# A decoder trunk on one Trainium2 core: down and output products as 2x2 blocks with seven block products

## The chip, the core and the metric

The kernel runs on one core of one Trainium2 chip. The metric is the device time of one execution in microseconds (us); the median of three runs of the kernel before is 1233.89 us (1233.36 to 1233.97). All shapes are fixed: 512 positions, model width 1024, FFN width 2816, 16 heads, fp32 inputs.

Engines are called PE (TensorE), DVE (VectorE), ACT (ScalarE), POOL (GpSimd) and SP (SyncE, whose queue issues the transfers). The built program holds a list of instructions for each engine; the pieces of these lists shown below are called order rows.

## The reference, cut to what matters

```python
def short_conv_mixer(xn, w_in, conv_w, w_out):
    b, c, h = jnp.split(xn @ w_in, 3, axis=-1)
    u = causal_dwconv(c * h, conv_w)
    return (b * u) @ w_out

def conv_ffn(xn, w_up, conv_w, w_down):
    a, g = jnp.split(xn @ w_up, 2, axis=-1)
    a = causal_dwconv(a, conv_w)
    return (jax.nn.silu(a) * g) @ w_down

# layer 0: x += short_conv_mixer(rmsnorm(x)); x += conv_ffn(rmsnorm(x))
# then shared K, V and a forget gate from rmsnorm(x)
# layer 1: x += forgetting_attention(q(rmsnorm(x)), k, v, c); x += conv_ffn(rmsnorm(x))
```

The products that the change rewrites are `@ w_out` of the mixer (1024x1024) and `@ w_down` of both FFNs (2816x1024), each on 512 positions.

## The kernel before

Everything is kept transposed: a tile has 128 channels on the partitions and 512 positions along the free dimension. The stages follow one another: the mixer's input product (24 output tiles from `a_in`), its output product (8 tiles from `a_out`), FFN 0's up product (22 values of j, for each a tile a and a tile g), its down product (8 output tiles, 22 blocks of K each), keys, values and attention, `b_out`, then FFN 1 in the same way.

fp32 products are made of fp32r passes. Each weight and each activation is split into a high part, rounded to fp32r, and a low part, the remainder. For each block of K of 128 and each half of 256 positions PE runs three matmuls of 128x256: high by high, high by low and low by high (`mac`, L130 to L132). So one output tile with 8 blocks of K (`gemm`) is 48 matmuls.

A piece of weights is loaded with 8 blocks of K (512 KB) into one of three buffers `wraw`. Then, 512 columns at a time, ACT rounds the high part (L110) and DVE subtracts it to get the low part (L111), into four buffers of a pool of their own, `wsp`. One gemm so has two casts on ACT and two subtractions on DVE. Activations are split by `split` (cast L162 on ACT, subtraction L163 on DVE or POOL).

In the up stage each j runs: gemm of a, L316 on DVE (a times the norm's factor r), the convolution (L241 on ACT, L242 and L244 on DVE), SiLU (L192 on ACT), gemm of g, L322 on DVE (g times r), L323 on POOL (g times y), and the split (L162, L163). The down stage then runs the 8 gemms with 22 blocks of K, and x is added by L271 on DVE. In the mixer, L292 to L302 play the part of L316 to L323, and x is written to DRAM (`xsp`) only after FFN 0's down stage, tile by tile.

Nobody writes the order of the queues by hand: a scheduler places the instructions, and it hands out the buffers of a pool in the order in which the program asks for them. In the program before, `wsp` belongs to the weights alone, and `f`-like products and their splits come from other pools.

Of the kernel before, what the change touches and what calls it, by code (L numbers as in the profile page):

```python
# [52 lines left out]
def trunk(ctx: ExitStack, tc: tile.TileContext, x_t, a_in, a_out, up0, down0, wk, wv, wf, wqg, b_out,  # L54
# [78 lines left out]

    def gemm(src, xs, nk=KT):

        ps = mmps()
        for k, w in enumerate(weights(src, nk)):
            mac(ps, w, xs[k], k == 0, k == nk - 1)
        return ps

    def gemm2(srcs, xs, hold=1):

        pss, kept = [], []
        for src in srcs:
            ps = mmps()
            late = []
            for k, w in enumerate(weights(src)):
                if k < KT - hold:
# [5 lines left out]
        for ps, late in zip(pss, kept):  # L154
            for k, w in late:
                mac(ps, w, xs[k], False, k == KT - 1)
# [80 lines left out]

    def conv(src, col):
# [9 lines left out]
    def back(m):  # L248
        t = new(misc, "ld", [P, T], F32, bufs=3)
        nc.sync.dma_start(out=t, in_=xsp[m])  # L250
        return t

    def project(src, hs, nk, norm, last=False, spilled=False, spill=False, pss=()):

        for m in range(KT):
            if m < len(pss):
                ps = pss[m]
            elif nk == KT and m < 2:
# [3 lines left out]
            else:  # L262
                ps = gemm(src[m], hs, nk)
# [615 lines left out]
```

## Time and profile before

| what | value |
| --- | --- |
| median of three runs | 1233.89 us (1233.36 to 1233.97) |
| the profiled execution's own time | 1233.1 us |
| span of the profiled execution, first to last instruction | 1231.3 us |
| PE busy | 1216.5 us, 99% of the span, 10425 matmuls |
| DVE, ACT, POOL busy | 678.6, 537.4 and 203.1 us |
| mean granted clock of TensorE | 0.996 |

A share of 99% for PE says that TensorE is nearly always at work over the whole program; the pipelined matmuls overlap in the records, so the length of one record is more than the distance from one matmul to the next. A granted clock of 1 is TensorE's upper level, 2.4 GHz, and 0.5 is 1.2 GHz. In a row of the timeline the first number is the start in the span, the second the duration, and the bracket at the end names the idle time before it and what ended it.

### The profile page before, as it was taken

Reading aid. Unit: us, or ns where it says so; the run is one execution under the profiler, and the core shown is the slowest. Engines: PE = TensorE matmul, PEld = TensorE weight load, DVE = VectorE, ACT = ScalarE, POOL = GpSimd, SP = SyncE. Lnnn points to the kernel's source line nnn. Section 1 sums busy time; section 2 is a strip of 40 time slices with the busy share of each in tenths; the row PEclk is TensorE's granted clock in tenths of the full one; section 3 lists DMA queues with packets and bytes.
Section 4 is the critical chain, followed back from the end, with each engine's and each line's share of the span. In section 5 each row is a group of like instructions: output and inputs, shape, how many; then the busy total and the mean of one; then the engine's idle time right before and its main releaser. Section 6 shows DMA issues by size and latency. Waiting matters only on the chain.

```text
span 1231.3 us, 24568 instructions
## 1 busy us (share of the span) xinstructions
PE 1216.5 (99%) x10425; PEld 1189.0 (97%) x10425; DVE 678.6 (55%) x1163; ACT 537.4 (44%) x973; POOL 203.1 (16%) x181
## 2 busy tenths in 40 slices
PE   9999999999999999999999899999999999999998
PEld 8999999999999999999998788889999999999998
DVE  6755556555555533344646787876565555553222
ACT  5433345334333433333556767775543334342221
POOL 0100021111111100000123435442111111110000
PEclk9999999999999999999999999999999999999999
DMA  6233233333333344342342212124233233233341
GB/s 215 87 103 101 88 104 92 97 104 93 97 104 91 93 130 125 121 140 87 95 139 79 84 52 86 53 87 129 86 104 101 89 103 101 89 99 104 116 119 45
DMA packets 39374, 124.14 MB, mean 101 GB/s; under 512 B 4384, under 2 KB 4896, under 8 KB 39264
## 3 DMA queue, kind: packets, MB, share of 16 engines
q1 hardware_dynamic: 38048, 120.41, 31.8%
q10 hardware_dynamic: 1152, 1.97, 0.5%
q8 instruction: 81, 1.33, 0.4%
q14 instruction: 29, 0.24, 0.1%
q0 software_dynamic: 64, 0.20, 0.0%
HBM read 118.33 MB, written 4.23 MB: 100 GB/s over the span
## 4 chain that ended last, share of the span: by engine, by line
PE 90%; ACT 4%; DVE 3%; POOL 2%; issue 1%; DMA 0%; SPq 0%; DVEq 0%; POOLq 0%; ACTq 0%
PE st L131 18%; PE st L130 17%; PE st L132 17%; PE mm L130 11%; PE mm L132 11%; PE mm L131 11%; ACT s L189 1%; PE st L620 1%; PE at L658 1%; PE st L649 1%; POOL m L667 1%; DVE s L624 1%; DVE wlo L111 1%; ACT g L189 1%; ACT g L162 1%
## 5 line engine op out<-in xcount | busy, mean ns | idle before, releaser
L130 PE MATMUL st<-g,whi 128*128 128x256 f32 x1686 | 465.5, 276 | 0.0
L131 PE MATMUL st<-g,whi 128*128 128x256 f32 x1686 | 465.4, 276 | 0.0
L132 PE MATMUL st<-g,wlo 128*128 128x256 f32 x1686 | 465.4, 276 | 0.0
L110 ACT CAST whi<-wraw 128x512 fp32r<-128x512 f32 (+1 forms) x394 | 240.4, 611 | 473.6 <-PE st L131 291.9
L111 DVE TENSOR_TENSOR wlo<-wraw,whi 128x512 fp32r<-128x512 f32 (+1 forms) x394 | 283.6, 720 | 222.9 <-ACT whi L110 218.3
L130 PE MATMUL mm<-g,whi 128*128 128x256 f32 x1242 | 346.2, 279 | 0.0
L131 PE MATMUL mm<-g,whi 128*128 128x256 f32 x1242 | 343.5, 277 | 0.0
L132 PE MATMUL mm<-g,wlo 128*128 128x256 f32 x1242 | 343.5, 277 | 0.0
L130 PEld LDWEIGHTS st<-g,whi 128*128 128x128 f32 x1686 | 316.6, 188 | 0.1
L131 PEld LDWEIGHTS st<-g,whi 128*128 128x128 f32 x1686 | 316.5, 188 | 0.1
L132 PEld LDWEIGHTS st<-g,wlo 128*128 128x128 f32 x1686 | 316.5, 188 | 0.0
L130 PEld LDWEIGHTS mm<-g,whi 128*128 128x128 f32 x1242 | 233.5, 188 | 1.8
L131 PEld LDWEIGHTS mm<-g,whi 128*128 128x128 f32 x1242 | 233.4, 188 | 1.3
L132 PEld LDWEIGHTS mm<-g,wlo 128*128 128x128 f32 x1242 | 233.2, 188 | 0.1
L323 POOL TENSOR_TENSOR m<-m,m 128x512 f32<-128x512 f32 x44 | 69.1, 1573 | 408.3 <-DVE m L322 370.9
L162 ACT CAST g<-m 128x512 fp32r<-128x512 f32 x66 | 40.8, 619 | 90.4 <-POOL m L323 66.8
L163 DVE TENSOR_TENSOR g<-m,g 128x512 fp32r<-128x512 f32 x51 | 36.8, 722 | 67.3 <-ACT g L162 66.7
L224 POOL TENSOR_TENSOR m<-m,m 128x512 f32<-128x512 f32 x21 | 27.9, 1330 | 175.5 <-ACT m L222 153.6
L640 POOL TENSOR_SCALAR s<-s,sm 128x128 f32<-128x128 f32 (+3 forms) x64 | 41.4, 660 | 75.5 <-DVE sm L637 69.2
L189 ACT ACTIVATE s<-s,bb 128x128 f32<-128x128 f32 (+3 forms) x64 | 35.4, 555 | 22.9 <-DVE bb L633 22.8
L241 ACT ACTIVATE m<-m,pr 128x512 f32<-128x512 f32 x52 | 37.7, 725 | 15.9 <-DVE m L316 13.0
L242 DVE SCALAR_TENSOR_TENSOR m<-m,pr,m 128x511 f32<-128x511 f32 x52 | 39.0, 750 | 9.5 <-ACT m L241 9.5
(170 smaller groups left out, 1312.3 us busy)
## 6 DMA issues: line engine op xcount, KB each, us to landing
wraw<-up SPq DMA_DIRECT2D x88, 512.0 KB, 3.5
wraw<-down SPq DMA_DIRECT2D x32, 448.0 KB, 3.5
wraw<-a_in SPq DMA_DIRECT2D x21, 512.0 KB, 3.6
wraw<-down SPq DMA_DIRECT2D x16, 512.0 KB, 3.5
wraw<-wqg SPq DMA_DIRECT2D x16, 512.0 KB, 3.6
wraw<-a_out SPq DMA_DIRECT2D x8, 512.0 KB, 3.5
ld<-xsp SPq DMA_DIRECT2D x16, 256.0 KB, 2.8
wraw<-wv SPq DMA_DIRECT2D x8, 512.0 KB, 3.6
```

Of the source, the lines that this page charges most:

```text
L110: nc.scalar.copy(out=hi[:, :n], in_=raw)
L111: nc.vector.tensor_tensor(out=lo[:, :n], in0=raw, in1=hi[:, :n].bitcast(F32), op=ALU.subtract)
L130: nc.tensor.matmul(ps[:, f], lhsT=lh[0], rhs=rh[0][:, f], start=go, stop=False, skip_group_check=True)
L131: nc.tensor.matmul(ps[:, f], lhsT=lh[0], rhs=rh[1][:, f], start=False, stop=False, skip_group_check=True)
L132: nc.tensor.matmul(ps[:, f], lhsT=lh[1], rhs=rh[0][:, f], start=False, stop=end, skip_group_check=True)
L162: nc.scalar.copy(out=hi, in_=src)
L163: (eng or nc.vector).tensor_tensor(out=lo, in0=src, in1=hi.bitcast(F32), op=ALU.subtract)
L189: chain["exp"] = ordered(nc.scalar.activation(**kw), chain["set"])
L241: nc.scalar.activation(out=y, in_=src, func=AF.Copy, scale=pr[:, col + 2:col + 3])
L242: nc.vector.scalar_tensor_tensor(out=y[:, 1:T], in0=src[:, 0:T - 1], scalar=pr[:, col + 1:col + 2], in1=y[:, 1:T], op0=ALU.mult, op1=ALU.add)
L323: nc.gpsimd.tensor_tensor(out=g, in0=g, in1=y, op=ALU.mult)
L640: nc.gpsimd.tensor_scalar(out=s, in0=s, scalar1=sm[:, e:e + 1], scalar2=1.0, op0=ALU.mult, op1=ALU.mult)
```

## The change

The three products become 2x2 block products in Winograd's form. Two K blocks of the activation (two tiles of j, or of i in the mixer) and the two halves of 256 positions give one operand of four blocks; two output tiles m and two K blocks of weights give the other. Seven block products, each of n pairs of K blocks, take the place of eight. For that

- `operands` makes from each pair of tiles, in the wide tile `f`, three sums of blocks on DVE (L250, L252, L253), and splits all of them (ACT L257 three times and L262, DVE L258 three times and L263);
- `Seven.prepare` makes the sums of the weights on POOL (L281 1024 or 768 columns wide, L283 and L284 half as wide) and splits raw weights and sums (ACT L290, DVE L291);
- `Seven.go` runs the products (L305 to L307), and the outputs are put together by copies on ACT (L318, L320, L324) and additions on POOL and DVE (L321, L325, L326, L335 to L337, L425);
- the down stage runs in three parts, with 3, 4 and 4 pairs, after the gemm of g of j=6 and j=14, and at the end. Between the parts x lies in DRAM: each part loads its tiles of x (`ld`) and stores the sum (`xsp`). `Project` prepares the first `Seven` of a part when it is made, ahead of the gemms of j=6, 14 and 21.

The pools `wraw`, `wsp`, `sp` and `ptp` become one pool `wide` of 18 tiles of 128x1024. Raw weights, their high and low parts, `f` and the sums `t` of `operands`, and tiles of the attention all come from it. Weights are split 1024 columns at a time (L113 on ACT, L114 on DVE, once per gemm instead of twice). In all gemms that stay, the matmuls are L131 to L133. Lines that have moved: L316 is now L484, L322 L490, L323 L496, L241 L343, L242 L344, L244 L346, L192 L195. The program has 10113 matmuls after 10425 before; those of 128x256 go from 9792 to 9480.

```diff
-    big = ctx.enter_context(tc.tile_pool(name="big", bufs=58))
-    sp = ctx.enter_context(tc.tile_pool(name="sp", bufs=10))
-    ptp = ctx.enter_context(tc.tile_pool(name="ptp", bufs=6))
+    big = ctx.enter_context(tc.tile_pool(name="big", bufs=52))
-    wraw = ctx.enter_context(tc.tile_pool(name="wraw", bufs=3))
-    wsp = ctx.enter_context(tc.tile_pool(name="wsp", bufs=4))
+    wide = ctx.enter_context(tc.tile_pool(name="wide", bufs=18))
...
+    def W(dtype=F32):
+        return new(wide, "w", [P, 2 * T], dtype)
...
-        hi = new(wsp, "whi", [P, T], F32R)
-        lo = new(wsp, "wlo", [P, T], F32R)
-        nc.scalar.copy(out=hi[:, :n], in_=raw)
-        nc.vector.tensor_tensor(out=lo[:, :n], in0=raw, in1=hi[:, :n].bitcast(F32), op=ALU.subtract)
+        hi, lo = W(F32R), W(F32R)
+        nc.scalar.copy(out=hi[:, :n], in_=raw[:, :n])
+        nc.vector.tensor_tensor(out=lo[:, :n], in0=raw[:, :n], in1=hi[:, :n].bitcast(F32), op=ALU.subtract)
...
+    def operands(f):
+        t, v = W(), blocks(f)
+        tv = blocks(t)
+        nc.vector.tensor_tensor(out=tv[:, 0:2], in0=v[:, 0:4:3], in1=v[:, 1:2].to_broadcast([P, 2, HT]),
+                                op=ALU.subtract)
+        nc.vector.tensor_tensor(out=tv[:, 2], in0=tv[:, 1], in1=v[:, 0], op=ALU.add)
+        nc.vector.tensor_tensor(out=tv[:, 3], in0=tv[:, 2], in1=v[:, 2], op=ALU.subtract)
+        ops = {}
+        for names, src in (("57", tv[:, 0:2]), ("13", v[:, 0:4:3]), ("64", tv[:, 2:4])):
+            hi, lo = G(F32R), G(F32R)
+            nc.scalar.copy(out=blocks(hi), in_=src)
+            nc.vector.tensor_tensor(out=blocks(lo), in0=src, in1=blocks(hi).bitcast(F32), op=ALU.subtract)
...
+        g = G(F32R)
+        nc.scalar.copy(out=g[:, 0:HT], in_=v[:, 2])
+        nc.vector.tensor_tensor(out=g[:, HT:T], in0=v[:, 2], in1=g[:, 0:HT].bitcast(F32), op=ALU.subtract)
...
+    class Seven:
...
+        def prepare(self):
+            b, (r0, r1) = self.b, self.raw
+            s, s2 = W(), W()
+            nc.gpsimd.tensor_tensor(out=blocks(s[:, 0:2 * b], b), in0=blocks(r0[:, 0:2 * b], b),
+                                    in1=blocks(r1[:, b:2 * b], b).to_broadcast([P, 2, b]), op=ALU.add)
+            nc.gpsimd.tensor_tensor(out=s2[:, 0:b], in0=s[:, 0:b], in1=r0[:, b:2 * b], op=ALU.add)
+            nc.gpsimd.tensor_tensor(out=s2[:, b:2 * b], in0=s2[:, 0:b], in1=r1[:, 0:b], op=ALU.add)
+            self.w = {}
+            for names, raw in (("14", r0), ("2", r1), ("75", s), ("63", s2)):
+                n = len(names) * b
+                hi = W(F32R)
+                lo = hi[:, n:2 * n] if len(names) == 1 else W(F32R)
+                nc.scalar.copy(out=hi[:, 0:n], in_=raw[:, 0:n])
+                nc.vector.tensor_tensor(out=lo[:, 0:n], in0=raw[:, 0:n], in1=hi[:, 0:n].bitcast(F32), op=ALU.subtract)
...
+        def go(self, names, xs, ks):
...
+            for m in names:
...
+                for p in ks:
...
+                    nc.tensor.matmul(ps, lhsT=wh, rhs=xh, start=m in "57" and p == 0, stop=False, skip_group_check=True)
+                    nc.tensor.matmul(ps, lhsT=wh, rhs=xl, start=False, stop=False, skip_group_check=True)
+                    nc.tensor.matmul(ps, lhsT=wl, rhs=xh, start=False, stop=p == self.n - 1, skip_group_check=True)
...
+    class Project:
+        def __init__(self, src, n):
+            self.src, self.n = src, n
+            self.sevens = {}
+            self.load(0)
+            self.load(1)
+            self.sevens[0].prepare()
...
         for j in range(JT):
+            if j in parts_ or j == JT - 1:
+                n = min(c for c in parts_ if c >= j) // 2 - k0
+                part = Project([z[:, 4 * k0 * P:4 * (k0 + n) * P] for z in down], n)
...
-            nc.gpsimd.tensor_tensor(out=g, in0=g, in1=y, op=ALU.mult)
-            if j < 5:
-                us.append(split(g, new(sp, "s", [P, T], F32R), new(sp, "s", [P, T], F32R)))
-            else:
-                us.append(split(g))
-        project(down, us, JT, nxt, last, spill=spill)
+            if j in parts_:
+                part.run(us, None)
+                us, k0 = [], k0 + n
+            if j % 2 == 0:
+                f = W()
+            nc.gpsimd.tensor_tensor(out=half(f, j), in0=g, in1=y, op=ALU.mult)
+            if j % 2:
+                us.append(operands(f))
+        part.run(us, nxt, last=last, hold=True)
```

**The end of an even j in the up stage.** DVE's order rows before, for the end of the gemm of g of one j (L322 waits for it) and the start of the next; `whi` and `wlo` are the halves of a weight piece, a new piece has a new `wraw`, and PE reads wlo_3290 in the first half of the next gemm.

```order
L111 TENSOR_TENSOR wlo_3290<-wraw_3287,whi_3289 128x512
L322 TENSOR_TENSOR m_3213<-st_3154,r_2405 128x512
L111 TENSOR_TENSOR wlo_3318<-wraw_3287,whi_3317 128x512
L163 TENSOR_TENSOR g_3217<-m_3213,g_3216 128x512
L111 TENSOR_TENSOR wlo_3356<-wraw_3353,whi_3355 128x512
L316 TENSOR_TENSOR m_3279<-st_3220,r_2405 128x512
```

The change, DVE, for the end of g of j=2 (L490) and the a of j=3, whose low part is w_2668; w_2730 is the low part of the g of j=3.

```order
L484 TENSOR_TENSOR m_2598<-mm_2543,r_2384 128x512
L344 SCALAR_TENSOR_TENSOR m_2600<-m_2598,pr,m_2600 128x511
L346 SCALAR_TENSOR_TENSOR m_2600<-m_2598,pr,m_2600 128x510
L490 TENSOR_TENSOR m_2660<-st_2605,r_2384 128x512
L114 TENSOR_TENSOR w_2668<-w_2665,w_2667 128x1024
L114 TENSOR_TENSOR w_2730<-w_2727,w_2729 128x1024
L484 TENSOR_TENSOR m_2719<-st_2664,r_2384 128x512
```

The low part of the next gemm's weights stood ahead of L322, and now stands behind L490.

**The end of an odd j.** DVE's order rows of the change from the end of g of j=3 (L490) on; w_2807 is the low part of the weights of the a of j=4, and w_2662 is `f`.

```order
L490 TENSOR_TENSOR m_2781<-st_2726,r_2384 128x512
L250 TENSOR_TENSOR w_2784<-w_2662 128x512
L252 TENSOR_TENSOR w_2784<-w_2784,w_2662 128x256
L253 TENSOR_TENSOR w_2784<-w_2784,w_2662 128x256
L258 TENSOR_TENSOR g_2789<-w_2784,g_2788 128x512
L258 TENSOR_TENSOR g_2793<-w_2662,g_2792 128x512
L258 TENSOR_TENSOR g_2797<-w_2784,g_2796 128x512
L263 TENSOR_TENSOR g_2800<-w_2662,g_2800 128x256
L114 TENSOR_TENSOR w_2807<-w_2804,w_2806 128x1024
L114 TENSOR_TENSOR w_2869<-w_2866,w_2868 128x1024
L484 TENSOR_TENSOR m_2858<-st_2803,r_2384 128x512
```

On ACT before, around the SiLU (L192) and the cast of one j's product (L162 into s_2688):

```order
L241 ACTIVATE m_2621<-m_2619,pr 128x512
L110 CAST whi_2761<-wraw_2759 128x512
L192 ACTIVATE m_2621<-m_2621 128x512
L110 CAST whi_2789<-wraw_2759 128x512
L162 CAST s_2688<-m_2685 128x512
L110 CAST whi_2827<-wraw_2825 128x512
L110 CAST whi_2855<-wraw_2825 128x512
```

On ACT in the change, from the convolution and SiLU (L343, L195) of j=3 on; w_2806 is the high part of the weights of the a of j=4, w_2868 that of its g.

```order
L343 ACTIVATE m_2721<-m_2719,pr 128x512
L195 ACTIVATE m_2721<-m_2721 128x512
L257 CAST g_2788<-w_2784 128x512
L257 CAST g_2792<-w_2662 128x512
L257 CAST g_2796<-w_2784 128x512
L262 CAST g_2800<-w_2662 128x256
L113 CAST w_2806<-w_2804 128x1024
L113 CAST w_2868<-w_2866 128x1024
L343 ACTIVATE m_2860<-m_2858,pr 128x512
```

Before, one cast L162 stood between the casts of weights; now the four casts of `operands`, of which the first and the third wait for DVE's L250 and L253, stand ahead of L113, and L250 waits for POOL's L496. In before, the DVE rows at this place are those of the even j, since each j is alike there.

**The entry of a part.** On POOL in the change, around j=5, whose product is the second L496 into w_2922; L281 to L284 into w_3071 and w_3072 are the sums of the first `Seven` of the part, those into w_3210 and w_3211 of the second. Before, POOL has only L323 here, one for each j.

```order
L496 TENSOR_TENSOR w_2922<-m_2920,m_2860 128x512
L496 TENSOR_TENSOR w_2922<-m_3041,m_2981 128x512
L281 TENSOR_TENSOR w_3071<-w_3063,w_3064 128x768
L283 TENSOR_TENSOR w_3072<-w_3071,w_3063 128x384
L284 TENSOR_TENSOR w_3072<-w_3072,w_3064 128x384
L281 TENSOR_TENSOR w_3210<-w_3067,w_3068 128x768
L283 TENSOR_TENSOR w_3211<-w_3210,w_3067 128x384
```

On DVE in the change, at the same place, from the last splits of `operands` on; w_3095 is the low part of the weights of the a of j=6, w_3157 that of its g.

```order
L258 TENSOR_TENSOR g_3057<-w_3044,g_3056 128x512
L263 TENSOR_TENSOR g_3060<-w_2922,g_3060 128x256
L291 TENSOR_TENSOR w_3077<-w_3063,w_3076 128x768
L291 TENSOR_TENSOR w_3080<-w_3064,w_3080 128x384
L291 TENSOR_TENSOR w_3084<-w_3071,w_3083 128x768
L291 TENSOR_TENSOR w_3088<-w_3072,w_3087 128x768
L114 TENSOR_TENSOR w_3095<-w_3092,w_3094 128x1024
L114 TENSOR_TENSOR w_3157<-w_3154,w_3156 128x1024
L291 TENSOR_TENSOR w_3216<-w_3067,w_3215 128x768
L291 TENSOR_TENSOR w_3219<-w_3068,w_3219 128x384
```

All four splits of the first `Seven`, of which the last two wait for POOL's sums, have come ahead of the next gemm's L114.

## Rows read from the trace of the kernel before

**Rows 1.** The page: span, busy times, chain by engine.
```profile
span 1231.3 us, 24568 instructions
PE 1216.5 (99%) x10425; PEld 1189.0 (97%) x10425; DVE 678.6 (55%) x1163; ACT 537.4 (44%) x973; POOL 203.1 (16%) x181
PE 90%; ACT 4%; DVE 3%; POOL 2%; issue 1%; DMA 0%; SPq 0%; DVEq 0%; POOLq 0%; ACTq 0%
```

**Rows 2.** Busy time of each engine in the up stage of FFN 0.
```profile
core 0: us, PE busy (x) PEld busy (x) DVE busy (x) ACT busy (x) POOL busy (x), PEclk, DMA share, GB/s
190.00:429.00 239.00, 239.00 (x2109) 238.91 (x2108) 135.82 (x201) 98.07 (x159) 34.57 (x22) 1.00 0.32 97
```

**Rows 3.** Timeline, DVE: outputs of the mixer, one for each gemm of 48 matmuls.
```profile
157.10 0.69 DVE L271 TENSOR_TENSOR g<-st,g 128x512 f32<-128x512 f32 x1 [0.56 <-PE st L132]
...
184.30 0.69 DVE L271 TENSOR_TENSOR g<-st,g 128x512 f32<-128x512 f32 x1 [1.44 <-PE st L132]
```

**Rows 4.** Groups by line and shape: count, busy us and mean ns, idle before.
```profile
L298 POOL TENSOR_TENSOR m<-m,r 128x512 f32<-128x512 f32 x8 | 10.6, 1328 | 127.2 <-DVE m L244 88.5 <-ACT whi L110 38.7
L640 POOL TENSOR_SCALAR s<-s,sm 128x512 f32<-128x512 f32 x16 | 15.6, 989 | 18.4 <-DVE sm L637 18.4
L640 POOL TENSOR_SCALAR s<-s,sm 128x128 f32<-128x128 f32 x16 | 5.8, 377 | 13.2 <-DVE sm L637 11.8 <-DVE mx L632 1.4
L110 ACT CAST whi<-wraw 128x512 fp32r<-128x512 f32 x362 | 224.0, 620 | 418.8 <-PE st L131 254.8 <-PE mm L131 134.3 <-ACT m L222 10.6
L110 ACT CAST whi<-wraw 128x384 fp32r<-128x384 f32 x32 | 16.4, 514 | 54.8 <-PE st L131 37.1 <-PE mm L131 17.7
L111 DVE TENSOR_TENSOR wlo<-wraw,whi 128x512 fp32r<-128x512 f32 x362 | 265.9, 735 | 192.7 <-ACT whi L110 188.1 <-PE st L131 2.0 <-PE mm L131 2.0
L111 DVE TENSOR_TENSOR wlo<-wraw,whi 128x384 fp32r<-128x384 f32 x32 | 17.7, 553 | 30.2 <-ACT whi L110 30.2
```

**Rows 5.** Timeline of PE, DVE, ACT and POOL in the up stage of FFN 0.
```profile
238.97 0.28 PE L130 MATMUL mm<-g,whi 128*128 128x256 f32 x1
...
239.17 0.69 DVE L322 TENSOR_TENSOR m<-mm,r 128x512 f32<-128x512 f32 x1 [1.44 <-PE mm L132]
239.78 0.68 DVE L111 TENSOR_TENSOR wlo<-wraw,whi 128x512 fp32r<-128x512 f32 x1
...
241.64 0.62 ACT L162 CAST s<-m 128x512 fp32r<-128x512 f32 x1 [1.97 <-POOL m L323]
242.17 0.61 ACT L110 CAST whi<-wraw 128x512 fp32r<-128x512 f32 x1
...
240.01 1.60 POOL L323 TENSOR_TENSOR m<-m,m 128x512 f32<-128x512 f32 x1 [9.28 <-DVE m L322]
```

**Rows 6.** Timeline of DVE and POOL: a subtraction that meets a POOL operation.
```profile
138.65 1.75 DVE L111 TENSOR_TENSOR wlo<-wraw,whi 128x512 fp32r<-128x512 f32 x1 [0.23 <-ACT whi L110]
...
138.56 1.29 POOL L298 TENSOR_TENSOR m<-m,r 128x512 f32<-128x512 f32 x1 [15.09 <-DVE m L244]
```

**Rows 7.** TensorE after idle time: at the start, around 705 us, and 700 to 720.
```profile
6.38 0.58 PE L130 MATMUL mm<-g,g 128*128 128x256 f32 x1 [0.58 <-ACT g L162]
...
9.35 0.41 PE L132 MATMUL st<-g,g 128*128 128x256 f32 x1
...
10.19 0.28 PE L130 MATMUL st<-g,g 128*128 128x256 f32 x1
...
707.95 1.00 PE L620 MATMUL st<-g,g 64*128 64x256 f32 x5 [3.38 <-DVE mx L624]
...
700.00:720.00 20.00, 16.62 (x118) 14.10 (x117) 14.13 (x38) 12.88 (x30) 8.81 (x12) 0.83 0.11 36
```

**Rows 8.** Timeline, SyncE's DMA queue, at the end of FFN 0's down stage.
```profile
530.03 10.61 SPq L372 DMA_DIRECT2D wraw<-wv  x3
544.53 0.33 SPq L277 DMA_DIRECT2D xsp<-g  x1
```

More of the change, by code (lines that the diff above doesn't have):

```diff
@@ L257, in project @@
                 ps = pss[m]
-            elif nk == KT and m < 2:
+            elif m < 2:
                 if m == 0:
@@ L277, in project, with __init__, load, run @@
                 nc.sync.dma_start(out=xsp[m], in_=x[m])
+    class Project:
+        def __init__(self, src, n):
+            self.src, self.n = src, n
[3 more added lines that the diff above has]
+            self.sevens[0].prepare()
+        def load(self, q):
+            if q < KT // 2:
+                self.sevens[q] = Seven(self.src[q], self.n)
+        def run(self, xs, norm, last=False, hold=False, old=None):
+            n = self.n
+            if hold:
+                self.sevens[1].prepare()
+                for q in (0, 1):
+                    self.sevens[q].early(xs, range(n - 1))
+            for q in range(KT // 2):
+                sv = self.sevens[q]
+                if q + 1 < KT // 2:
+                    if not (hold and q == 0):
+                        self.sevens[q + 1].prepare()
+                    self.load(q + 2)
+                if not hold or q > 1:
+                    sv.early(xs, range(n))
+                elif q == 0:
+                    for q2 in (0, 1):
+                        self.sevens[q2].early(xs, (n - 1,))
+                sv.late(xs)
+                self.end(q, sv, norm, last, old)
+        def end(self, q, sv, norm, last, src):
+            l, r = slice(0, HT), slice(HT, T)
+            m0, m1 = 2 * q, 2 * q + 1
+            old = [back(m, src) for m in (m0, m1)]
+            for m in (m0, m1):
+                x[m] = G()
+            o0 = added(sv, old, (x[m0], x[m1]))
+            if last:
+                nc.scalar.dma_start(out=out_t[m1], in_=x[m1])
+            if last and q == KT // 2 - 1:
+                for f, eng in ((r, nc.scalar), (l, nc.sync)):
+                    nc.vector.tensor_tensor(out=x[m0][:, f], in0=sv.b0[:, f], in1=o0[:, f], op=ALU.add)
+                    eng.dma_start(out=out_t[m0][:, f], in_=x[m0][:, f])
+            else:
+                nc.vector.tensor_tensor(out=x[m0], in0=sv.b0, in1=o0, op=ALU.add)
+                if last:
+                    nc.sync.dma_start(out=out_t[m0], in_=x[m0])
+            for m in (m0, m1):
+                if norm is not None:
+                    norm.add(m)
+                if not last:
+                    nc.sync.dma_start(out=xsp[m], in_=x[m])
+    def half(f, k):
+        return f[:, (k % 2) * T:(k % 2 + 1) * T]
     def mixer(norm, nxt, first):
@@ L300, in mixer, with ffn @@
                 pb = gemm(a_in[i, 2], norm.xs)
-            b = M()
-            nc.vector.tensor_tensor(out=b, in0=pb, in1=u, op=ALU.mult)
-            bu.append(split(b))
-        project(a_out, bu, KT, nxt)
-    def ffn(up, down, col, norm, nxt, last=False, spill=False):
+            if i % 2 == 0:
+                f = W()
+            nc.vector.tensor_tensor(out=half(f, i), in0=pb, in1=u, op=ALU.mult)
+            if i % 2:
+                bu.append(operands(f))
+        out.run(bu, nxt, hold=True, old=x_t)
+    def ffn(up, down, col, norm, nxt, last=False):
         r = None
-        us = []
+        us, parts_ = [], [6, 14, JT]
+        k0 = 0
         for j in range(JT):
+            if j in parts_ or j == JT - 1:
+                n = min(c for c in parts_ if c >= j) // 2 - k0
+                part = Project([z[:, 4 * k0 * P:4 * (k0 + n) * P] for z in down], n)
             if j == 0:
@@ L747, in attention @@
         fill(2 * KT)
-        w2 = list(weights(b_out[2]))
+        w2 = list(weights(b_out[2], 0, KT))
         ps2 = bank("st")
@@ L837 @@
         arrays[f"up{l}"] = np.stack([u[0], u[1]], axis=1)
-        arrays[f"down{l}"] = tiles(inp["ffn_w_down"][l])
+        arrays[f"down{l}"] = pairs(inp["ffn_w_down"][l], (0, 3, 7, JT // 2))
     wkvf = inp["w_kvf"]
```

138 lines of the change are left out of this document (92 added, 46 removed).

## The prediction

> **What bounds the kernel now.** I read the page first. PE is busy in 1216.5 us of a span of 1231.3, the other engines in at most 55% of it, and PE holds 90% of the chain that ended last [rows 1]. Then the busy times by stretch: in the up stage PE is busy in all 239.00 us at full clock, DVE in 135.82 and ACT in 98.07 [rows 2]. So whatever shortens PE's list shortens the time, as long as PE waits for nothing; and whatever makes it wait is paid in full, since it has no slack elsewhere. Last the timelines, for prices. PE never waits at the end of a j, because the halves of the next gemm's weights are ready before the last gemm ends. That is a property of the order of the lists, and the order is what I compare below.
>
> **What the change removes.** 312 matmuls of 128x256 fewer (9792 to 9480). Six gemms of 48 matmuls lie between outputs at 157.10 and at 184.30 [rows 3], five distances in 27.20 us: 5.44 us a gemm, 0.1133 us a matmul. 312 x 0.1133 = **-35.3 us**.
>
> **Prices.** POOL: an addition 512 wide takes 1.33 us [rows 4]. Wider ones are not in the trace: from 512 up by the slope of the L640 rows, (989-377)/384 = 1.59 ns a column, or in proportion, a 768 takes 1.74 to 1.99, a 1024 2.14 to 2.66; a 384 1.0 to 1.13. So one `prepare` holds POOL for 3.7 to 4.3 us with three pairs, 4.8 to 5.3 with four. ACT: (620-514)/128 = 0.83 ns a column [rows 4], so 1.04 us for 1024, 0.83 for 768, 0.41 for 256. DVE: 0.68 us for an undisturbed 512 [rows 5]; with the 553 ns of the 384 [rows 4] that is 1.0 ns a column: 1.2 us for 1024 (1.36 in proportion), 0.94 for 768, 0.42 for 256. From POOL to ACT it takes 0.03 us (240.01+1.60 to 241.64), and a DVE result starts 0.20 after the start of the matmul that follows the gemm (238.97 to 239.17) [rows 5].
>
> **End of an even j.** The third matmul of the next gemm needs its low part, L114, and that now stands behind L490, which waits for the gemm that ends. L490 runs from 0.20 to 0.89 after PE could have gone on, L114 takes 1.2 more: 2.1, less the two matmuls that PE has (0.2): 1.9 us (1.7 to 2.0). Eight such ends in each FFN: 16 x 1.9 = **30 us**.
>
> **End of an odd j.** L490 to 0.89, L496 on POOL 1.03 to 2.33, then L250 to 3.05, L252 to 3.5, L253 to 3.95. On ACT the casts L257 follow: the first behind L250, the third from 4.1 to 4.75, L262 to 5.1, and only then L113, to 6.1. DVE has done L258 and L263 by then; L114 ends at 7.3. PE had two matmuls: it waits 7.2 us (6.3 if every step overlaps the next as consecutive L111s do, 8.0 with L496 at 1.60 [rows 5]). Eight in each FFN: 16 x 7.2 = **115 us**. What is queued behind the waiting instructions is the next gemm's weights on both ACT and DVE, so no other engine can feed PE meanwhile.
>
> **Entry of a part.** At j=5 the four splits of the first `Seven` come between `operands` and L114. DVE alone: 2.4 until L496 is done, 3.95 for `operands`, 0.94+0.55+0.94+0.94 for the splits, 1.2 for L114: 10 us, with steps that overlap 9, less 1.2 of matmuls. But DVE and POOL also meet: the subtraction of 0.68 took 1.75 beside L298's 1.29, which it started 0.09 after [rows 6], so the two had to go one after the other. Then POOL's 3.7 to 4.3 is added, and some of the second `Seven`'s sums: 14.5 us (9 to 16). With four pairs at j=13 sums and splits are a third longer: 16.5 (10 to 18.5). At j=20 there is no `operands`, but POOL's 4.8 to 5.3 behind L496, ACT 1.04, and two DVE steps of 1.2: 10.3 without meeting, I take 11.5 (10 to 12.5). At the end of the up stage about 15 us of operands, second sums and splits stand against 72 matmuls, 8.2 us, that need only the older pairs: 7 (0 to 8). j=6 and j=14 cost nothing: their weights are split during the part's products. 14.5+16.5+11.5+7 = 49.5, twice: **99 us**.
>
> **Mixer.** The product comes from DVE, so the odd ends lack POOL's leg (7.2-1.4 = 5.8) and there are three, three even ones at 1.9, an entry at i=6 (8.8, as j=20 less the wider cover), and 2 at the end: **34 us** (25 to 38).
>
> **Inside the parts, and after them.** 28 `Seven`s, in each of which PE's later products wait for a copy or for sums that meet DVE: 0.5 us each, 15 in all (5 to 30). Two tiles come at once and late to the norm's squares: 11 more for the mixer, FFN 0 and the end (0 to 15). One loss on SP: before, three loads of `wv` are issued from 530.03, ahead of the store of the last tile of x at 544.53 [rows 8]; now two stores that wait for that tile stand ahead of the first load of `wv`, so V begins a landing, a cast and a subtraction late: **6 us**. Stores and loads of x themselves cost nothing otherwise: they run behind products of many us. Sum of this part: **32 us**.
>
> **The clock.** After idle time PE runs on the lower level. At the start matmuls of 0.41 us stand from 6.38 to 10.0, and 0.28 from 10.19 on; after an idle 3.38 us at 707.95, the mean clock of 700 to 720 is 0.83 [rows 7]. The first is 3.6 us at half speed, 1.8 lost; the second loses up to 0.17 x 20 = 3.4. By my steps there are 29 waits of over 5 us (16 odd ends, 8 in the parts, 4 in the mixer, V): 29 x 2.0 = **58 us** (0 to 99). The Trainium skill, "TensorE: Matmul & The Clock Gate", Part 1, ties the clock to how busy PE has been, which agrees with these rows.
>
> **Sum.** -35 + 30 + 115 + 99 + 34 + 32 + 58 = +333 us. On the profiled execution's 1233.1 (1.8 over its span) that is 1566; the median is 0.8 higher: **1567 us**. The low ends give -35+27+101+58+25+10 = +186 without any loss of clock (1420), about +230 with the 1.8 at 24 waits; the high ends -35+32+128+110+38+51+99 = +423 (1657).
>
> Were ready splits able to pass the waiting ones, the two kinds of ends, 145 us, and the clock's part of the sixteen longer ones, 32, would go, and 1390 be left. The rows show L110 at 242.17 behind the L162 that waited for POOL until 241.64 [rows 5]; they do not show whether it could have gone sooner. By the Trainium skill, "PSUM — Partial Sum Buffer", section "Engine vs sequencer instructions", the queues of these engines are strictly first in, first out; by that, 1567 stands.
>
> **Rivals.**
> *The waits come as I say, but the clock stays up*, since stalls are spread: 1567-58 = 1509. Against it speaks that a shorter idle time than 7.2 us was followed by a lower clock [rows 7]. 15%.
> *POOL's sums alone count:* the ends of j are covered in a way that I overlook, and only entries, products and V cost: 1234-35+99+32 = 1330, with the clock's part of 9 waits 1350. For it speaks that POOL is the slowest engine for an addition [rows 4]. The Trainium skill, "GPSIMD Engine Reference", section 4.1, sends elementwise work to VectorE and not to GPSIMD; that is this rival's rule. 6%.
> *Faster:* PE stays fed, as now in the up stage [rows 2], and the matmul count decides: 1234-35 = 1199, up to 1215 with waits in the parts. It would need L490 plus L114, 1.9 us, to lie under matmuls that PE already can run, at each of the 42 ends; from about 0.8 us a wait the gain is gone. 3%.
> *No difference:* waits that happen to give back the 35 us: 1%.
>
> **How the numbers follow.** Forecast 75%, so 1567. A measurement of this kernel can tell about 0.2% from no change. Range: from the first rival's neighbourhood with low ends (1440) to near the high ends (1640); it leaves out the 10% of the last three rivals and the tails of the first two. Faster 3%, same 1%, slower 96%.
>
> **What would show it.** In the profile after, PE idle before L133 and before L131 with DVE L114 and ACT L113 as releasers, some 1.9 us and 7 us long in turn after each g; PE busy near 80% of the span; each FFN, up and down together, longer by 120 to 160 us; PEclk below 1.0 after each longer wait; DVE's L258 and L291 means above 0.7 and 0.95 where POOL adds. I am wrong if L114 runs before the gemm ahead has ended, or if PE's idle time lies mainly within L305 to L307.

## The result

The changed kernel takes 1672.06 us (median of four runs, 1667.92 to 1672.33) against 1233.62 before: 1.355 times as long, with a 95% interval of 1.3525 to 1.3577. The forecast was slower, 1567 us, with a range up to 1640; the direction was right and the size too small by 105 us.

The page of the changed kernel, with the lines that answer to [rows 1], and its clock in 40 slices:

```profile
span 1670.1 us, 24358 instructions
PE 1325.0 (79%) x10113; PEld 1265.0 (76%) x10113; DVE 888.3 (53%) x1232; ACT 582.8 (35%) x960; POOL 445.7 (27%) x349
PE   7888776678866887686999989997669786877768
PEclk9899888789987989778999999998879888888879
```

PE has 312 matmuls fewer and is busy for 108.5 us longer, and it idles for 345 us, where before it idled for 15. The span is longer by 438.8. Who PE waits for shows the view of waits (engine, line, what it waited for: us in total, times, longest):

```profile
PE st L131 <- ACT w L113: 97.0, 15, 11.3
PE mm L131 <- ACT w L113: 70.3, 11, 11.3
PE mm L305 <- ACT w L290: 41.6, 4, 11.2
PE st L133 <- DVE w L114: 31.3, 27, 3.1
...
PE mm L133 <- DVE w L114: 12.6, 15, 1.7
```

L131 and L133 are the plain gemms, L305 and L306 the seven products. More than 200 us are waits of plain gemms for the casts (L113) and subtractions (L114) of their own weights, which they did not wait for before. The end of an odd j in the timeline, PE first, then DVE, ACT and POOL (the last matmul of g is that at 290.84):

```profile
290.84 0.28 PE L133 MATMUL mm<-g,w 128*128 128x256 f32 x1
296.98 0.58 PE L131 MATMUL mm<-g,w 128*128 128x256 f32 x1 [5.86 <-ACT w L113]
...
298.24 0.58 PE L133 MATMUL mm<-g,w 128*128 128x256 f32 x1 [0.47 <-DVE w L114]
...
291.16 0.69 DVE L490 TENSOR_TENSOR m<-mm,r 128x512 f32<-128x512 f32 x1 [2.64 <-PE mm L133]
293.29 0.69 DVE L250 TENSOR_TENSOR w<-w 128x512 f32<-128x512 f32 x1 [1.44 <-POOL w L496]
294.02 0.42 DVE L252 TENSOR_TENSOR w<-w,w 128x256 f32<-128x256 f32 x1
294.48 0.42 DVE L253 TENSOR_TENSOR w<-w,w 128x256 f32<-128x256 f32 x1
294.82 1.89 DVE L258 TENSOR_TENSOR g<-w,g 128x512 fp32r<-128x512 f32 x3
...
296.96 2.36 DVE L114 TENSOR_TENSOR w<-w,w 128x1024 fp32r<-128x1024 f32 x2
...
294.02 1.66 ACT L257 CAST g<-w 128x512 fp32r<-128x512 f32 x3 [4.77 <-DVE w L250]
295.58 0.40 ACT L262 CAST g<-w 128x256 fp32r<-128x256 f32 x1
295.89 1.99 ACT L113 CAST w<-w 128x1024 fp32r<-128x1024 f32 x2
...
292.00 1.26 POOL L496 TENSOR_TENSOR w<-m,m 128x512 f32<-128x512 f32 x1 [15.85 <-DVE m L490]
```

The chain is the one that the order rows led to: L490, POOL's L496, L250 to L253, the casts L257 and L262, and only then the first L113 (295.89, two in one row), behind which L131 starts at 296.98, and L133 waits once more for L114, until 298.24. The windows show how long that lasts:

```profile
core 0: us, PE busy (x) PEld busy (x) DVE busy (x) ACT busy (x) POOL busy (x), PEclk, DMA share, GB/s
290.00:300.00 10.00, 3.67 (x20) 3.17 (x19) 6.66 (x10) 3.86 (x6) 1.26 (x1) 0.66 0.32 102
300.00:310.00 10.00, 10.00 (x76) 10.00 (x76) 2.19 (x3) 1.45 (x3) 0.00 (x0) 0.83 0.16 57
310.00:320.00 10.00, 8.31 (x73) 8.12 (x73) 4.74 (x4) 2.06 (x3) 2.13 (x1) 1.00 0.15 52
```

From 290 to 310 the granted clock is 0.66 and 0.83, and in the third window, with a wait of 1.69 us at the end of an even j, it is 1.00.

The start of an FFN and the entry of a part, with PE's first matmul after the wait, and what went ahead of it on ACT, DVE and POOL:

```profile
275.79 0.58 PE L131 MATMUL st<-g,w 128*128 128x256 f32 x1 [10.21 <-ACT w L113]
...
266.34 0.63 ACT L192 ACTIVATE m<-v 128x512 f32<-128x512 f32 x1 [4.76 <-DVE v L237]
...
270.50 0.72 ACT L343 ACTIVATE m<-m,pr 128x512 f32<-128x512 f32 x1 [2.21 <-DVE m L484]
...
274.17 0.63 ACT L195 ACTIVATE m<-m 128x512 f32<-128x512 f32 x1
274.70 1.98 ACT L113 CAST w<-w 128x1024 fp32r<-128x1024 f32 x2
...
366.11 0.58 PE L305 MATMUL mm<-g,w 128*128 128x256 f32 x1 [9.60 <-ACT w L290]
...
358.67 2.27 DVE L250 TENSOR_TENSOR w<-w 128x512 f32<-128x512 f32 x1 [1.44 <-POOL w L496]
360.98 1.10 DVE L252 TENSOR_TENSOR w<-w,w 128x256 f32<-128x256 f32 x1
...
358.60 1.80 POOL L281 TENSOR_TENSOR w<-w,w 128x768 f32<-128x768 f32 x1
360.47 1.33 POOL L283 TENSOR_TENSOR w<-w,w 128x384 f32<-128x384 f32 x1
```

At the start, L113 for the a of j=1 (274.70) stands behind SiLU (L195), and that behind the norm's factor (in this kernel L192 is a step of it): 10.21 us, in a place where the prediction had an even end of 1.9. At the entry at j=5, L250 took 2.27 us beside L281, where it takes 0.69 alone (at 293.29 above). It ended at 360.94, 0.54 after L281's end (360.40): DVE and POOL do go one after the other, as in [rows 6].

**Where 438.8 us come from.** The 312 matmuls give back 35.3. PE's idle time is 330 us more (the gaps between its records, 339.8 less 9.5). PE's busy time is 1325.0 in place of 1216.5 - 35.3 = 1181.2, 144 more. The trace's record of the clock has 46 stretches at half speed in which PE worked, and PE was busy in them for 230 us (before, 2 stretches, 8.8 us): half of the difference, 111 us, is the lower clock. The other 33 are what is left; I put them down to the ends and beginnings of the pipelined matmuls, since there are 113 more gaps of over 0.1 us than before, 0.29 us for each, and two runs below give nearly the same price. -35.3 + 330 + 111 + 33 = 439.

### The profile page after: what moved, and what is told of

The parts are those of the page before. It is cut to its first block, busy times and chain, and to the rows that moved or that the text cites. A ratio compares the mean times of both kernels' runs of the same rounds, so it can differ in the third digit from the quotient of the medians.

```text
span 1670.1 us, 24358 instructions
## 1 busy us (share of the span) xinstructions
PE 1325.0 (79%) x10113; PEld 1265.0 (76%) x10113; DVE 888.3 (53%) x1232; ACT 582.8 (35%) x960; POOL 445.7 (27%) x349
## 5 line engine op out<-in xcount | busy, mean ns | idle before, releaser
L131 PE MATMUL st<-g,w 128*128 128x256 f32 x1280 | 373.5, 292 | 97.0 <-ACT w L113 97.0
L133 PE MATMUL st<-g,w 128*128 128x256 f32 x1280 | 373.6, 292 | 31.3 <-DVE w L114 31.3
L132 PE MATMUL st<-g,w 128*128 128x256 f32 x1280 | 370.2, 289 | 0.0
L131 PE MATMUL mm<-g,w 128*128 128x256 f32 x976 | 287.8, 295 | 73.3 <-ACT w L113 70.3
L131 PEld LDWEIGHTS st<-g,w 128*128 128x128 f32 x1280 | 257.8, 201 | 100.4 <-ACT w L113 100.4
L133 PE MATMUL mm<-g,w 128*128 128x256 f32 x976 | 284.9, 292 | 12.6 <-DVE w L114 12.6
L133 PEld LDWEIGHTS st<-g,w 128*128 128x128 f32 x1280 | 255.4, 200 | 38.1 <-DVE w L114 38.0
L132 PE MATMUL mm<-g,w 128*128 128x256 f32 x976 | 283.1, 290 | 0.0
L132 PEld LDWEIGHTS st<-g,w 128*128 128x128 f32 x1280 | 257.5, 201 | 0.2 <-DVE g L172 0.2
L131 PEld LDWEIGHTS mm<-g,w 128*128 128x128 f32 x976 | 196.3, 201 | 77.8 <-ACT w L113 72.7
L496 POOL TENSOR_TENSOR w<-m,m 128x512 f32<-128x512 f32 x44 | 69.2, 1573 | 602.3 <-DVE m L490 477.9
L114 DVE TENSOR_TENSOR w<-w,w 128x1024 fp32r<-128x1024 f32 x141 | 193.8, 1400 | 44.3 <-ACT w L113 43.9
L133 PEld LDWEIGHTS mm<-g,w 128*128 128x128 f32 x976 | 195.6, 200 | 16.5 <-DVE w L114 16.5
L132 PEld LDWEIGHTS mm<-g,w 128*128 128x128 f32 x976 | 196.8, 202 | 1.2
L343 ACT ACTIVATE m<-m,pr 128x512 f32<-128x512 f32 x52 | 37.6, 724 | 429.5 <-DVE m L484 334.4
L291 DVE TENSOR_TENSOR w<-w,w 128x1024 fp32r<-128x1024 f32 (+1 forms) x112 | 150.6, 1368 | 51.4 <-ACT w L290 50.0
L305 PE MATMUL st<-g,w 128*128 128x256 f32 x460 | 138.4, 303 | 36.7 <-ACT m L318 21.6
L113 ACT CAST w<-w 128x1024 fp32r<-128x1024 f32 x141 | 142.5, 1043 | 30.4 <-DMA w<-up 11.6
L306 PE MATMUL st<-g,w 128*128 128x256 f32 x460 | 135.4, 295 | 4.8 <-DVE g L258 4.8
L307 PE MATMUL st<-g,w 128*128 128x256 f32 x460 | 134.7, 295 | 3.9 <-DVE w L291 3.8
L290 ACT CAST w<-w 128x1024 fp32r<-128x1024 f32 (+1 forms) x112 | 96.3, 887 | 115.1 <-POOL w L284 38.5
L305 PE MATMUL mm<-g,w 128*128 128x256 f32 x268 | 84.2, 315 | 55.1 <-ACT w L290 41.6
```

Of the source, the lines that this page charges most:

```text
L113: nc.scalar.copy(out=hi[:, :n], in_=raw[:, :n])
L114: nc.vector.tensor_tensor(out=lo[:, :n], in0=raw[:, :n], in1=hi[:, :n].bitcast(F32), op=ALU.subtract)
L131: nc.tensor.matmul(ps[:, f], lhsT=lh[0], rhs=rh[0][:, f], start=go, stop=False, skip_group_check=True)
L132: nc.tensor.matmul(ps[:, f], lhsT=lh[0], rhs=rh[1][:, f], start=False, stop=False, skip_group_check=True)
L133: nc.tensor.matmul(ps[:, f], lhsT=lh[1], rhs=rh[0][:, f], start=False, stop=end, skip_group_check=True)
L290: nc.scalar.copy(out=hi[:, 0:n], in_=raw[:, 0:n])
```

## The experiments

Two theories stood against each other. **Places:** PE waits because the splits of the next weights stand behind `f` and `t` in the lists, and they do because all these tiles come from one pool, whose buffers are handed out in the program's order. **POOL:** the sums on POOL, and their meeting DVE, hold everything up. All runs but two are the changed kernel with one edit or a few.

### The order alone, in the kernel before

Two runs of the kernel before. The low part of the next a's weights is made to stand behind DVE's multiplication of g (`e3a`), or its casts and low parts behind the whole split of the product on ACT and DVE (`e3b`). No pool, size or product differs.

```diff
+ with ExitStack() as es:
+     for b in behind:        # e3a: the product with r; e3b: cast and subtraction of the split
+         es.enter_context(tc.issue_after(b.ins))
      pa = gemm(up[j, 0], norm.xs)
```

> The kernel before, with only the order changed: in both up stages the low part of the next a's weights stands behind the multiplication of this g by r on DVE, as at the change's even ends. Nothing else differs. Theory: 42 waits of 0.89 + 0.68 - 0.2 = 1.3 us, 55 us, and the clock stays up, as after the 1.7 us waits of the changed kernel: about 1290. Rival (any wait of this kind brings the lower clock): some 2 us more at each, 1370. Rival (order matters only with the shared pool): 1234.

> The kernel before, with only the order changed: in both up stages the casts and subtractions of the next a's weights stand behind the whole split of this j's product, on ACT and on DVE. Theory: the chain is 0.89 for the product with r, 1.4 on POOL, 0.62 and 0.69 for the split and 0.68 for the low part, less 0.2 of matmuls: 42 waits of 4.2 us = 176 us, and the lower clock after each, at 2.2 to 2.5 us a time as in the changed kernel: 92 to 105 more. About 1505. Rival (the clock's part belongs to the seven products and not to the waits): 1410.

Measured: 1297.32 and 1507.63 us (one run each, before 1233.64), where Places had 1290 and 1505. PE's busy time and what it waited for, first with the low part late, then with both:

```profile
PE 1232.6 (95%) x10425; PEld 1197.0 (92%) x10425; DVE 713.8 (55%) x1163; ACT 546.1 (42%) x973; POOL 201.7 (16%) x181
...
PE st L132 <- DVE wlo L111: 35.5, 28, 5.7
PE mm L132 <- DVE wlo L111: 13.0, 14, 0.9
```

```profile
PE 1323.2 (88%) x10425; PEld 1277.4 (85%) x10425; DVE 674.4 (45%) x1163; ACT 529.2 (35%) x973; POOL 189.0 (13%) x181
...
PE st L130 <- ACT whi L110: 111.5, 28, 11.8
PE mm L130 <- ACT whi L110: 47.3, 14, 3.4
```

In `e3a` two of the 42 waits, at the starts of the FFNs, are of 5.7 us and the other 40 of 0.9; PE's busy time is 16 us more than the 1216.5 of before. In `e3b` the two are of 11.8 us and the other 40 of 3.4; PE is busy for 107 us more, for the same 10425 matmuls. The record of the clock has two more stretches at half speed in `e3a` than before, after the two long waits, and 42 more in `e3b`, one after each wait. That is 4 of the 16 us and 87 of the 107; the rest, 12 us over 42 more gaps of over 0.1 us and 19 over 69, is 0.28 us a gap in both. So the order alone, without seven products, costs 274 us, and here the waits of 3.4 us brought the lower clock while those of 0.9 did not. The rival that ties the clock to the seven products falls.

### Requesting the weights early

`e1` requests the weights of the next a ahead of the product of this g, at the 16 ordinary ends. `e2` does so at all ends, at the entries, at the starts and in the mixer.

```diff
+ wa = ask(up[j + 1, 0])      # list(weights(...)): load, cast, subtraction
  g = M()
  nc.vector.tensor_tensor(out=g, in0=pg, in1=r, op=ALU.mult)
...
- pa = gemm(up[j, 0], norm.xs)
+ pa = gemm(up[j, 0], norm.xs, ws=wa)
```

> The changed kernel, with the weights of the next a requested in the program ahead of the product of this g, at the 16 ordinary ends of j in the two up stages; pools, work and sizes stay. Theory (the waits come from where the splits stand in the lists): the waits of 1.7 us at even ends and 6.3 us at odd ends go, of the odd ones about 1.5 us stays, since the weights of the next g still stand behind the operands. 8 x 2 x 1.7 + 16 x 4.8 + the clock's part of the 16 long ones (2.5 us each) = 144 us off 1672: about 1528. Rival (the pool of 18 wide tiles is full, so that splits wait for free tiles wherever they are requested): over 1630. Rival (additions on POOL meet DVE and hold everything up): over 1630 too, since all of that work stays.

> As the run on the ordinary ends, and in addition the next weights are requested early at the start of each FFN (ahead of the norm's factor), at the entries of the parts (a and g ahead of the first sums), at the odd ends for g too, and in the mixer. Theory: the starts (2 x 10.9 us), the entries (2 x 35 us), the mixer's waits (35 us), the rest of the odd ends (24 us) and the clock's part of some 20 waits (50 us) go as well: 1528 - 202 = about 1325, where what is left above 1199 are waits inside the parts, at V and at the norms. Rival (POOL and the order inside the parts carry most of the loss): over 1420. If the matmul count decided at once, 1200.

Measured: 1513.66 us (two runs; ratio to before 1.227, 1.2233 to 1.2308) and 1388.92 us (1.1249, 1.1218 to 1.128). The first is 158 us below the change, 14 more than expected; nothing but the place of the requests differs, so the pool was not short of tiles at these ends. The second is 64 us above what was expected. What PE still waits for in it (L308 is the first matmul of a product there, and the L131 rows are the starts):

```profile
PE mm L131 <- ACT w L113: 16.6, 4, 5.8
PE st L308 <- ACT m L321: 14.0, 3, 7.6
PE st L308 <- ACT w L293: 13.1, 3, 8.3
...
PE mm L308 <- ACT w L293: 12.1, 2, 8.3
```

At the starts a1 came early, but g1 was not requested early and now waits up to 5.8 us; and products wait up to 8.3 us for casts of their own weights, at the entries, and up to 7.6 for copies. Both sit in the parts, where I had left POOL's sums as they were.

### The sums on DVE

`e4` has the early requests of `e2` and `e8` has none; in both, the three sums of `prepare` run on DVE.

```diff
- nc.gpsimd.tensor_tensor(out=s2[:, 0:b], in0=s[:, 0:b], in1=r0[:, b:2 * b], op=ALU.add)
+ nc.vector.tensor_tensor(out=s2[:, 0:b], in0=s[:, 0:b], in1=r0[:, b:2 * b], op=ALU.add)
```

> The kernel with all next weights requested early (1389 us), with the sums of the weights on DVE in place of POOL. In that kernel a POOL sum and a DVE operation with two tiles as input still meet at the entries (three splits of operands took 3.5 to 4.1 us in place of 1.9). Theory (places in the lists decide, the engine of the sums little): 1365 to 1385, since the entries get shorter by 1 to 3 us each, and DVE takes 2.5 us more for each of 36 Sevens, mostly beside PE. Rival (POOL's sums and their meeting DVE carry most of what is left above 1199): 1330 or less. Rival (DVE becomes the bound inside the parts): over 1400.

> The changed kernel with one thing altered: the sums of the weights on DVE in place of POOL. All splits stand where they stood in the change. With the next weights requested early, this edit gave 42 us (1389 to 1347). Theory (in the change itself the ends of j, which have no sums, and the starts carry most): the entries fall by 1 to 3 us each and some waits in the parts go, 20 to 45 us: 1627 to 1652. Rival (POOL and its meeting DVE carry most of the loss in the change): below 1550.

Measured: 1347.19 us (1.0935, 1.0913 to 1.0957), 42 below `e2`, and 1618.78 (1.3131, 1.3102 to 1.3159), 53 below the change. (There are 28 Sevens, not the 36 of the first expectation.) Both lie below what Places expected, by 18 and 8 us. `e8` is far from POOL's figure (below 1550); `e4` lies as near to POOL's (1330 or less) as to Places'. So the sums on POOL cost more than I had thought, 42 and 53 us, but that is about an eighth of the loss of 438; the early requests of `e2` had taken 283.

### Two edits that did not help

`e5` takes `e2` and requests the norm's work on a Seven's tiles behind the next Seven's first products; `e6` takes `e2` and makes each part's `Project` one j earlier, and requests g1 and the mixer's first products early; `e7` has both.

> The kernel with all next weights requested early (1389 us), with the norm's work on the tiles of one Seven requested only behind the first products of the next, so that on ACT the copies that free PSUM for PE no longer stand behind scalings that wait for the finished x. Theory: the waits of 7.6 and 0.7 us in the mixer's product and in the last part of FFN 0 go, and the lower clock behind them: 2 x (8.3 + 2.5) = 22, less some 5 at the end of each, where more of the norm's work is left for the last Seven: 1370 to 1378. Rival (these waits come from POOL's additions that finish x, whatever stands ahead of the copies): 1385 to 1392.

> The kernel with all next weights requested early (1389 us), with each part's first weights and sums requested one j earlier, and the first g of each FFN and the first products of the mixer requested ahead of the norm's factor too. Theory: the waits at the starts (2 x 6 and 7 us) and at the two first entries of each FFN (2 x 21 us, of which perhaps 15 go each) fall, with the clock's part of some 7 waits (2.5 each): 12 + 5 + 30 + 17 = 64: about 1325. Rival (18 wide tiles are too few to hold a part's weights any earlier): 1370 or more.

> The norm's work later and the entries earlier, in one kernel. Theory: both savings add up, 1389 - 15 - 64 = 1310. It would still be slower than the kernel before, since the waits inside the parts, at V and in the last parts stay. If what is left were in the seven products themselves, nothing below 1340 would come.

Measured: 1390.24, 1425.55 and 1421.15 us. `e5` gained nothing, as its rival had it (the same edit gives 10 us below, in `f1`, where the sums are on DVE), and `e6` and `e7` are slower than `e2` by 37 and 32 us. In `e6` the waits at the starts fell, in the FFNs from 6.1 and 6.3 us to 1.5 and 1.4 and in the mixer from 7.3 to 4.6, but at the entry of the last part a plain gemm waits for its cast again, and the same at the other FFN:

```profile
568.75 0.58 PE L131 MATMUL mm<-g,w 128*128 128x256 f32 x1 [7.09 <-ACT w L113]
...
565.26 2.50 ACT L293 CAST w<-w 128x512 fp32r<-128x512 f32 x3
567.66 1.04 ACT L113 CAST w<-w 128x1024 fp32r<-128x1024 f32 x1
```

The part's tiles (L293), requested a j earlier from the shared pool, now stand ahead of that gemm's (L113): the first cause in a new place. My expectation had the saving and not what was pushed back. The time also lies in the range of the rival that 18 tiles are too few; no run with more tiles tells the two apart.

### A pool of their own for f and t

No order is asked for here; only where two kinds of tile come from.

```diff
- wide = ctx.enter_context(tc.tile_pool(name="wide", bufs=18))
+ wide = ctx.enter_context(tc.tile_pool(name="wide", bufs=15))
+ pairp = ctx.enter_context(tc.tile_pool(name="pairp", bufs=3))
...
- t, v = W(), blocks(f)
+ t, v = F(), blocks(f)       # F: a tile of pairp; f = F() in ffn and mixer
```

> The changed kernel with one thing altered: the tiles f and t of the operands come from a pool of their own with 3 tiles, and the pool of wide tiles has 15 in place of 18, the same memory. No order is asked for in the program. Theory (buffers of a pool are handed out in the program's order, and because f and t shared the weights' pool the next weights could not be split before f was written): the splits stand ahead again, also at the entries and the starts: 1672 - 144 - 24 (ends) - 50 (entries) - 33 (starts) - 15 (mixer) - 35 (the clock's part of the rest) = about 1370, down to 1300 if the parts' own weights come early too. Rival (the position of the splits comes from the order of the program text, or from the wide split of 1024): as the change, over 1600. Rival (15 tiles are too few): over 1500.

> The pool of their own for f and t, and the sums of the weights on DVE. Theory: both causes apart, so the saving of 42 us by DVE's sums comes on top in part (20 to 40): about 1335, between 1270 and 1350. Rival (the two are one cause: once splits stand ahead, POOL's sums are covered): as the run with the pool alone, within 8 us. Faster than the kernel before only if the waits inside the parts and at V were small, which I don't expect.

Measured: 1322.94 us (1.0715, 1.0676 to 1.0754), and with the sums on DVE 1273.43 (1.0335, 1.0311 to 1.0359). What PE waits for in the first, and in the second with a piece of ACT's timeline:

```profile
PE 1231.4 (93%) x10113; PEld 1190.8 (90%) x10113; DVE 867.4 (65%) x1232; ACT 586.5 (44%) x960; POOL 432.9 (33%) x349
...
PE st L309 <- ACT m L322: 18.4, 5, 5.9
PE mm L309 <- ACT m L322: 11.8, 4, 6.0
```

```profile
PE 1213.6 (95%) x10113; PEld 1172.7 (92%) x10113; DVE 874.6 (69%) x1316; ACT 587.0 (46%) x960; POOL 285.0 (22%) x265
...
PE st L309 <- ACT m L322: 8.4, 4, 4.8
PE mm L309 <- ACT m L322: 7.1, 4, 4.9
...
165.16 0.72 ACT L175 ACTIVATE g<-g,pr 128x512 fp32r<-128x512 f32 x1 [3.46 <-DVE g L429]
167.44 0.35 ACT L322 COPY m<-st 128x256 f32<-128x256 f32 x1
```

No plain gemm is among the first rows any more. 349 us, four fifths of the loss, go with the pool of three, within what Places expected (1300 to 1370), so the rival that the wide splits or the program's text set the order falls. The sums on DVE take 50 more, where I had 20 to 40, so the rival that the two are one cause falls as well. PE's busy time in the second is 1213.6, 32 above 1181.2; by the record of the clock 14 of these are the lower clock, where it was 111 in the change. The largest rows left are copies (L322) that free a product's bank: at 167.44 the copy stands behind the norm's scaling, which waited for x until 165.16.

### What is left

Four runs build on that kernel, each on the one before it: the norm's work late (`f1`), V's first weights ahead of the stores of x as well (`f3`), and 2 and 16 tiles in place of 3 and 15 (`f4`). The fourth (`g1`) requests the casts of the next Seven behind this Seven's copies.

> The kernel with a pool of its own for f and t and the sums on DVE (1273 us), with the norm's work on the tiles of one Seven requested behind the first products of the next. Theory (the two waits of 4.9 us in the mixer's product and in FFN 0's last part come from ACT's copies standing behind the norm's scalings): both go, with their part of the clock, 2 x (4.9 + 2) = 14: 1258 to 1264. Rival (as with POOL's sums, where the same edit gave nothing, the wait only moves to the end of the part): 1270 to 1275.

> In addition the first two pieces of V's weights are loaded and split before the last products of FFN 0, ahead of the stores of its last x. Theory: V's first 96 matmuls then stand ahead of the norm's two, and the waits of 5.8 and 1.2 us there go, with the clock's part of 2: 9 us less than with the norm's work alone, about 1252. Rival (V waits for the scaled x, not for its weights): within 3 us of the run before it.

> As the run before it, with 2 tiles for f and t and 16 wide ones in place of 3 and 15. Theory (f of the next pair is not written before t of the last one is split, so 2 hold the order back again only where a pair ends): the odd ends wait some us again, 1260 to 1300. Rival (the weights' tiles are the scarce ones): 1240 to 1250.

> The kernel with the pools of 2 and 16 tiles, the sums on DVE, the norm's work late and V's weights early (1250 us), with one thing altered: the casts and subtractions of the next Seven's weights are requested behind the copies of this Seven's first products, not ahead of them; its sums stay ahead. Theory (the 15 or so waits of 0.4 to 2.2 us inside the parts are PE waiting for ACT copies that stand behind casts which wait for DVE's sums): 8 to 14 us off, 1236 to 1242. Rival (then the splits come too late for the next products): 1250 or more. Below the kernel before only if the lower clock went too.

Measured: 1263.38, 1251.55 (1.0149, 1.0109 to 1.0188), 1250.48 and 1248.98 us (1.0124, 1.0083 to 1.0165). The first two came as Places expected, with a wide spread in the first (1259.64 to 1267.12). The third did not: 1260 to 1300 was expected, but 2 tiles for `f` and `t` do as well as 3. Fewer or more were not tried. The fourth missed as well (1236 to 1242 expected) and changed nothing that can be told from zero. PE in `f3`:

```profile
PE 1202.3 (96%) x10113; PEld 1163.9 (93%) x10113; DVE 873.0 (70%) x1316; ACT 587.2 (47%) x960; POOL 290.2 (23%) x265
...
PE st L815 <- POOL g L170: 6.3, 4, 3.1
PE st L309 <- DVE m L329: 4.3, 3, 1.8
```

PE is busy for 1202.3 us and idles for 47; the largest row is a wait in the attention. No version is faster than the kernel before. In `f3` 35 us of matmuls are saved and 53 are paid: 32 in idle time (small waits in 28 Sevens, some in the attention) and 21 in busy time, of which about 5 are the lower clock. Which of the waits a better order would take away stays open.

## Why the prediction was right in direction and too small

- **What bounds the kernel, and the matmuls saved.** Right: PE without slack, and 312 x 0.1133 us. `f3` has a busy time of 1202, near the 1181 that this leaves.
- **End of an even j: 1.9 us, 30 in all.** Right: 1.69 of idle time and the slower restart; with the starts taken out there are 14 of them, 24 us.
- **End of an odd j: 7.2 us, 115 in all.** Right: L133 starts 7.29 us after PE could have gone on (290.95 to 298.24), where I had 7.3. Of that PE idles 5.86 + 0.47 us, 101 in all, since the two matmuls between take longer at the lower clock than the 0.2 that I took off, which the clock's part below holds. (7.3 less 0.2 is 7.1, not the 7.2 that I charged: 2 us in all.)
- **Entries: 99 us.** Measured 78. Meeting of DVE and POOL is real (2.27 for 0.69), but fell on fewer operations: 10.3 and 9.9 at j=5 where I took 14.5, 12.1 and 11.6 at j=13 for 16.5; j=20 took 12.0 for 11.5, the end 5.3 for 7. (The steps that I listed for j=5 also add up to 10.9 on DVE alone, not 10.)
- **Mixer: 34 us.** Its ends and its entry took 30.
- **A place that the sum did not have: the starts.** At j=0 I counted an even end. There the next weights stand behind the whole calculation of the norm's factor, and in the mixer too: 11.1, 10.9 and 10.9 us, 33 in all.
- **Inside the parts, V, norms: 32 us.** Measured 55, two waits of 7.6 us among them, where copies stood behind the norm's work. Waits in the attention added some 8 that I had not counted.
- **The clock: 29 x 2.0 = 58 us. This is the term that failed.** It charged only waits of over 5 us. 29 such waits came, but that the number agrees is chance: 23 are among those that I had listed (16 odd ends, 6 entries of parts, the mixer's entry), and 6 are not (three starts, two waits of 7.6 us for copies, 5.8 at a norm). The record has 46 stretches at half speed in place of 29. The other 17 followed shorter waits, which I had left at nothing or listed as longer: 4.5 us at the mixer's three odd ends, waits of 1.2 to 3.2 us, mostly close together, inside the parts and at the end of the up stages (9), and 1.2 to 3.0 between the FFNs (5, where the kernel before has 2). At 2.4 us each the clock cost 111 us, above even my high end of 99; the price at the kernel's start (1.8), from which I came to 2.0, was near the low end of what [rows 7] allowed.
- **The restart of the pipelined matmuls, which no term held.** About 33 us over 113 gaps.
- **How that makes 105 us.** All waits together were 310 by my terms and 330 measured, so the sum of the waits was nearly right, in part because entries that were too long stand against starts that were not there. 20 for the waits, 53 for the clock and 33 for the restart are 106. The range stopped at 1640, though my own high ends came to 1657; the measured 1672 lies above both.
- **Rivals.** The clock does not stay up: in `e3b` waits alone, without seven products, cost 107 us of busy time, 87 of them at the lower clock. POOL's sums alone do not make the loss, but 42 to 53 us of it are theirs. In the Trainium skill, "GPSIMD Engine Reference", section 4.1, elementwise work belongs on VectorE; the runs with the sums on DVE agree (1389 to 1347, 1672 to 1619, 1323 to 1273). That ready splits could pass the waiting ones is not borne out: L113 stands behind L262 in the timeline above, and "PSUM — Partial Sum Buffer" of the Trainium skill, section "Engine vs sequencer instructions", says that these queues are first in, first out, which the run with only the order changed (1234 to 1508) agrees with.

## What to carry to other kernels

Before costing a saved operation, look at what the next stage's inputs stand behind in each engine's list, after a change that merges pools above all: a tile that is requested late and written late holds back every later request to its pool. Give tiles that wait for a result a pool apart from the prefetched ones; here three buffers moved gave back 349 of 438 us. And price a wait on TensorE with its lower clock and its restart: in `e3b`, at 40 waits of 3.4 us and two of 11.8, these added 107 / 42 = 2.5 us each.

## What was not expected of the hardware

What a wait does to the clock is not told by its length alone: 1.69 us of idle time at the even ends left it at 1.00, while in the attention a wait of 1.67 us and inside the parts one of 2.15 us were followed by half speed. DVE's additions that met POOL's sums ended only behind them: L250 took 2.27 us for 0.69 and ended 0.54 after L281, L252 took 1.10 for 0.42 and ended 0.28 after L283. And a gap between matmuls cost about 0.28 us of TensorE's time beyond the idle time and the clock, the same in three kernels (0.28, 0.28 and 0.29).
